# TensorE's instructions keep the order of the source, with grouped column-tiled products, from the second projection on

## The chip, the cores and the metric

One core of one Trainium2 chip runs the kernel. The metric is the device time of one execution in microseconds (us). Engines are named as the profile names them: PE is TensorE's matmul, PEld its weight load, DVE is VectorE, ACT is ScalarE, POOL is GpSimd, SP is SyncE, which here issues most DMAs.

## The reference

The input is x[1,256,1024]: 256 tokens, 1024 features, fp32. Two blocks run one after the other.

- The first block has one layer: an adaptive shift, scale and gate from a condition vector (the "ada" products); a state-space mixer (SSD, 32 heads in 4 groups, two chunks of 128 tokens); a sparse attention (NSA, 16 heads, with a compressed, a selected and a window branch); a gated sum of both; a router with 32 experts in 4 groups, two experts a token; a last RMS norm.
- The second block has two layers and a second sequence of 256 context tokens. Layer 0 is a grouped attention (16 heads on 4 key heads) of x over context and x, and of the context over itself, with a convolutional feed-forward for both. Layer 1 is a latent attention (MLA) of x over context and x with a feed-forward for x. A last RMS norm gives the output [1,256,1024].

```python
def first_block(...):                      # _hybrid_layer, one layer
    hn = _rmsnorm(h, norm1_g) * (1 + scale1) + shift1
    y_ssm = _mamba2_mixer(hn @ w_z, hn @ w_xbc, hn @ w_dt, ...) @ w_ssm_out
    y_nsa = _nsa_mixer(hn @ w_q, ..., hn @ w_gn, ...) @ w_nsa_out
    merged = sigmoid(hn @ w_gs) * y_ssm + sigmoid(hn @ w_ga) * y_nsa
    h = h + gate1 * (merged @ w_o)
    h = h + gate2 * _hier_moe(_rmsnorm(h, norm2_g) * (1 + scale2) + shift2, ...)
...
def mla_mixer(...):
    cq, ckv, k_rope = split(h @ w_in, [384, 640])
    q = rms_norm(cq, q_norm_g) @ w_uq
    kv = rms_norm(ckv, kv_norm_g) @ w_ukv
...
```

## The kernel before, in words

**Products.** Activations lie in SBUF feature-major, 128 features by 256 tokens a block. A product in nearly full fp32 precision is three matmuls in the type fp32r (`mm3`, lines 217 to 219): ACT casts a weight block to its high part (`whi`, line 198), DVE subtracts it for the low part (`wlo`, line 199), and PE adds high by high, low by high and high by low. `lin_fm` (line 221) keeps the weights stationary and streams 256 tokens; `lin_tm` keeps the activations stationary and streams up to 512 weight columns. These three lines, called the linear products below, are most of PE's work. Weights come by DMA on SP's queue into a ring of 14 buffers.

**Column- and row-tiled products.** Some products use only a part of the 128 by 128 array, and several of them sit side by side in it: the ada products (`ada_quad`, line 391) are four products of 32 columns each, written as a group of four for each of 8 slices of the weights; the experts' products (lines 1320 and 1342), the compressed scores (line 897) and the compression (line 850) are of the same kind. Attention's weighted sums (lines 989 and 1501) are pairs of 64 columns, its scores (944, 1690, 1713) pairs of 64 rows. Below, a burst is a run of such products with nothing of another kind, and not the same tile again, in between.

**The order.** The kernel is built on Tile, which collects the instructions of all engines and sets each engine's order itself, from its own estimate of when operands and buffers are ready; the order of the source sets only the priorities. The source is written as generators that `weave` and `mix` (lines 137 to 158) interleave: a main generator of linear products yields an estimated cost after each step, and fill generators (SSD, NSA, ada, attention, router) get a share of that cost. So the source has an interleaving of its own, in which a group is written whole; Tile's order before departs from it.

**The stages**, in order: the first projections (`first_act`, `project_tm`), the SSD's and convolution's inputs ("xbc"), the gates with SSD and NSA woven in (`ssd`, `nsa_compress` at line 832, `nsa_cmp_probs` at 890, `nsa_attend`), the two mixers' output products, the router, the experts with the context's attention and feed-forward of layer 0 woven in, then layer 0 for x (`layer0_x_attend`), its feed-forward with layer 1's context part, and layer 1 (`layer1_x`) with `mla_norm` (line 1741), `mla_kv_heads` and `mla_q_heads` and an attention (`attend`, line 1453) over them. `finish` makes the last norm. In `mla_norm` ACT copies a product out (line 1765) and squares it (1746), DVE and POOL make the reciprocal root (1747, 1749), DVE scales (1750) and PE transposes (1754). In a norm of x (`square_sums`, line 479) PE adds the squares up (491, 496), DVE and POOL make the root, PE broadcasts it (521), DVE and ACT make the normed activations (466 to 468), and the linear products follow.

**Buffers** that matter: PSUM has 8 banks. The first block gives 2 to the linear products, 1 to the ada products (`fl`), 2 to scores (`S`), 2 to `aux`, 1 to `acc`; the experts' stage 2, 2 (`S`), 2, 2; the layers of the second block 4 (`lin`, also the scores), 1, 2, 1.

Of the kernel before, what the change touches and what calls it, by code (L numbers as in the profile page):

```python
# [98 lines left out]
class Kernel:  # L99
# [915 lines left out]
    def tanh_gates(self, act, c0, sg):  # L1015
# [2 lines left out]
            self.A.activation(sg[:, m, :], ps, AF.Tanh, scale=0.5)  # L1018
        yield from self.lin_fm(self.I["w_in"][0], c0, D, act, ev)

    def mark(self, name):
        self.marks.append(name)

    def first_block(self, rb):
        V, A, T, I = self.V, self.A, self.T, self.I
        h = self.h
        act, pss = self.first_act(rb)
        self.mark("tm")
        self.drain(self.project_tm(act, pss))
        self.rope_tables()  # L1030
        self.ssd_dt()
        self.mark("xbc")
        self.load_vecs([3, 4, 5, 6, 7])
        for i in range(2):
            self.take_bias(self.fetch_bias(self.I["ada_b_2"][i]), self.ada2[i])
        prep = self.nsa_prepare()
        self.mix(self.project_xbc(act), (prep, 0.1))
        self.drain(prep)

        def nsa():  # L1040
            yield from self.nsa_compress()
            self.nsa_cmp_probs()
            yield 2.0
            yield from self.nsa_attend()
        ssg = self.sb("F", [P, 8, TOK], name="ssg")
        nsa_g, ssd_g, ada_g = nsa(), self.ssd(), self.ada_rest
        self.mark("ssg")
        self.mix(self.tanh_gates(act, 6992, ssg), (ssd_g, 0.7), (nsa_g, 0.35), (ada_g, 0.3))
        sga = self.sb("G", [P, 8, TOK], name="sga")
        self.mark("sga")  # L1050
        self.mix(self.tanh_gates(act, 8016, sga), (ssd_g, 0.6), (nsa_g, 0.35), (ada_g, 0.3))
        self.drain(ssd_g)
        self.mark("z")
        sums = [self.sb(f"cbm{i}", [P, 2, TOK], name="sums") for i in range(2)]
        self.mix(self.ssd_gate(act, sums), (nsa_g, 0.55), (ada_g, 0.3))
        self.drain(nsa_g)
        self.mark("norm")

        def ev_a(m, ps):
            V.scalar_tensor_tensor(sga[:, m, :], sga[:, m, :], 1.0, ps, OP.add, OP.mult)  # L1060
        norm = self.ssd_norm(sums)
        self.mix(self.lin_fm(I["w_nsa_out"][0], 0, D, self.nsa, ev_a), (norm, NORM), (ada_g, 0.2))
        self.drain(norm)
        self.mark("out")

        class Two:
            def __init__(self, ts):
                self.ts = ts

            def __getitem__(self, key):  # L1070
                _, k, s = key
                return self.ts[k // 8][:, k % 8, s]

        mh, ml = self.pair("B", [P, 8, TOK])

        def ev_s(m, ps):
            V.scalar_tensor_tensor(ssg[:, m, :], ssg[:, m, :], 1.0, ps, OP.add, OP.mult)
            V.tensor_tensor(sga[:, m, :], sga[:, m, :], ssg[:, m, :], OP.add)
            self.evict_split(mh[:, m, :], ml[:, m, :], sga[:, m, :])
        self.mix(self.lin_fm(I["w_ssm_out"][0], 0, D, (Two(self.y_hi), Two(self.y_lo)), ev_s), (ada_g, 0.3))  # L1080
        self.drain(ada_g)
        ctx = self.layer0_ctx_in()
        next(ctx)
        g = self.sb("s", [P, 8])
        V.tensor_scalar(g, self.ada1[:, 0, 16:24], 0.5, None, OP.mult)
        self.mix(self.residual(I["w_o"][0], (mh, ml), h, g), (ctx, CTXIN))
        self.drain(ctx)
        self.dbg("h1", h)
# [807 lines left out]
    def run(self):  # L1896
        with self.tc.tile_pool(name="sb", bufs=1) as self.pool:
            self.setup()
            self.h = self.sb("hx", [P, 8, TOK])
            self.ada1 = self.sb("ada1", [P, 1, 48])  # L1900
            self.ada2 = [self.sb(f"ada2{i}", [P, 2, 48]) for i in range(2)]
            for tag in SHARED:
                if tag == SHARED[tag]:
                    self.sb(tag, [P, 8, TOK])
            with self.phase(cw2=2, pb=5, pT=2), self.banks(lin=2, fl=1, S=2, aux=2, acc=1):
                first = [self.fetch_vecs(0)]
                x = self.fetch_tm(self.I["x"][0], "C", self.A)
                self.take_vecs([0], first)
                self.ada_stat()
                bias = self.fetch_bias(self.I["b_ada"][0])  # L1910
                first = [self.fetch_vecs(1)]
                self.turn_fm(x, self.h)
                self.load_constants(0)
                rb = self.sb("rb", [P, TOK])
                self.V.tensor_copy(rb, self.rms_bcast(self.h, 8, D))
                self.take_vecs([1], first)
                self.take_bias(bias, self.ada1)

                def rest():
                    yield from self.ada_first([1, 2])  # L1920
                    yield from self.ada_second(0)
                self.ada_rest = rest()
                self.first_block(rb)
            with self.phase(k4=4, m=3, fg=2, hT=2):
                with self.banks(lin=2, S=2, aux=2, acc=2):
                    self.load_constants(1)
                    self.mark("router")
                    ctx = self.layer0_ctx()
                    ada = self.ada_second(1, Q2)
                    self.mix(self.router(self.h), (ctx, 0.8), (ada, 0.5))  # L1930
                    self.drain(ada)
                    self.mark("experts")
                    self.mix(self.experts(), (ctx, 2.1))
                    self.mark("ctx rest")
                    self.drain(ctx)
                    self.mark("experts rest")
                    self.experts_rest()
                with self.banks(lin=4, fl=1, aux=2, acc=1):
                    self.mark("L0")
                    ada = self.ada_second(1, Q3)  # L1940
                    self.mix(self.layer0_x_attend(), (ada, 0.2))
                    self.drain(ada)
                    self.mark("L0 rest")
                    ctx = self.layer1_ctx()
                    self.mix(self.layer0_x_rest(), (ctx, 0.4))
                    self.drain(ctx)
                    self.mark("L1")
                    self.drain(self.layer1_x())
                    self.finish()


# [29 lines left out]
```

## Time and profile before

| | before |
|---|---|
| median of 3 runs | 1777.28 us (1777.13 to 1778.43) |
| the profiled execution | 1775.68 us, of it the profile's span 1773.9 us |
| PE busy | 1686.6 us (95%) |
| PEld busy | 1385.2 us (78%) |
| DVE busy | 1274.2 us (72%) |
| ACT busy | 913.8 us (52%) |
| POOL busy | 43.9 us (2%) |
| DMA | 381.54 MB, mean 215 GB/s |

A busy share is an average over stages with different limits. The stages lie in the profile at about these times: first projections to 78 us, xbc to 142, gates with SSD and NSA to 395, output products to 516, router to 577, context attention and experts to 1021, layer 0's projection to 1088, its attention to 1168, its feed-forward with layer 1's context to 1415, layer 1's latent projections to 1446, its attention to 1541, its feed-forward and the last norm to the end.

### The profile page before, as it was taken

The numbers are of one execution on the slowest core, as the hardware profiler recorded it, in microseconds if no ns is written. First come the engines' busy times: TensorE is split into PE (matmuls) and PEld (weight loads), VectorE is DVE, ScalarE is ACT, GpSimd is POOL, SyncE is SP. The second block draws the span as 40 slices with busy tenths as digits, with TensorE's granted clock in tenths as the row PEclk, the third lists the DMA queues.
The fourth block names the chain that finished last, engine by engine and source line by source line (L and its number), as shares of the span: only waits on it lengthen the run. The fifth ranks groups of instructions, "written<-read, shape, count | busy, mean of one in ns | idle before, by whom it ended". The sixth has DMA issues, their size and how long they took to land. (4 is left out here: it accounts for less than half of the span.)

```text
span 1773.9 us, 36446 instructions
## 1 busy us (share of the span) xinstructions
PE 1686.6 (95%) x12980; PEld 1385.2 (78%) x12980; DVE 1274.2 (72%) x3070; ACT 913.8 (52%) x1897; POOL 43.9 (2%) x48
## 2 busy tenths in 40 slices
PE   7999999999998999999999988999999989999998
PEld 3898767767876569888887644588999876789997
DVE  3997588566567677767666466968777788767876
ACT  2665445763443444434434253656665566556654
POOL 0000000010001000000000011000000000000000
PEclk9999999999999999999999989999999989989999
DMA  8756855847956897999999977334666432246662
GB/s 306 225 149 208 292 182 177 265 150 239 320 169 240 276 328 240 335 322 293 315 350 341 314 265 247 105 120 138 176 183 183 141 120 72 56 140 182 183 184 73
DMA packets 344962, 381.54 MB, mean 215 GB/s; under 512 B 27353, under 2 KB 298454, under 8 KB 344774
## 3 DMA queue, kind: packets, MB, share of 16 engines
q1 hardware_dynamic: 339456, 376.47, 67.7%
q10 hardware_dynamic: 5174, 1.97, 0.4%
q8 instruction: 104, 1.70, 0.4%
q14 instruction: 84, 0.69, 0.1%
q0 software_dynamic: 144, 0.71, 0.1%
HBM read 378.00 MB, written 1.05 MB: 214 GB/s over the span
## 5 line engine op out<-in xcount | busy, mean ns | idle before, releaser
L198 ACT CAST whi<-raw 128x512 fp32r<-128x512 f32 (+2 forms) x752 | 454.5, 610 | 403.5 <-PE lin L219 198.3
L199 DVE TENSOR_TENSOR wlo<-raw,whi 128x512 fp32r<-128x512 f32 (+2 forms) x752 | 503.8, 680 | 165.7 <-ACT whi L198 156.2
L217 PE MATMUL lin<-XA,whi 128*128 128x256 f32 x768 | 220.9, 288 | 1.4 <-ACT XA L467 1.4
L219 PE MATMUL lin<-XA,whi 128*128 128x256 f32 x768 | 219.6, 286 | 0.0
L218 PE MATMUL lin<-XA,wlo 128*128 128x256 f32 x768 | 219.4, 286 | 0.0
L217 PE MATMUL lin<-A,whi 128*128 128x256 f32 x576 | 167.8, 291 | 3.6 <-DVE k L600 1.9
L218 PE MATMUL lin<-A,wlo 128*128 128x256 f32 x576 | 164.6, 286 | 0.5 <-DVE wlo L199 0.5
L217 PEld LDWEIGHTS lin<-XA,whi 128*128 128x128 f32 x768 | 150.1, 195 | 2.7 <-ACT XA L467 2.5
L218 PEld LDWEIGHTS lin<-XA,wlo 128*128 128x128 f32 x768 | 149.7, 195 | 0.5 <-issue 0.4
L219 PEld LDWEIGHTS lin<-XA,whi 128*128 128x128 f32 x768 | 149.7, 195 | 0.3
L217 PEld LDWEIGHTS lin<-A,whi 128*128 128x128 f32 x576 | 110.6, 192 | 24.6 <-ACT whi L198 10.2
L219 PE MATMUL lin<-A,whi 128*128 128x256 f32 x448 | 128.5, 287 | 0.0
L217 PE MATMUL lin<-CA,whi 128*128 128x256 f32 x416 | 120.8, 290 | 0.0
L218 PE MATMUL lin<-CA,wlo 128*128 128x256 f32 x416 | 118.3, 284 | 0.0
L219 PE MATMUL lin<-CA,whi 128*128 128x256 f32 x416 | 118.0, 284 | 0.0
L218 PEld LDWEIGHTS lin<-A,wlo 128*128 128x128 f32 x576 | 110.7, 192 | 3.2 <-issue 1.6
L1624 ACT ACTIVATE cv<-lin,vecs 128x256 f32<-128x256 f32 x132 | 74.1, 561 | 62.0 <-PE lin L219 51.8
L219 PE MATMUL lin<-XB,whi 128*128 128x256 f32 x352 | 99.4, 286 | 0.1
L217 PE MATMUL lin<-XB,whi 128*128 128x256 f32 x352 | 98.7, 283 | 0.0
L218 PE MATMUL lin<-XB,wlo 128*128 128x256 f32 x352 | 98.4, 283 | 0.0
L1625 DVE SCALAR_TENSOR_TENSOR cv<-lin,vecs,cv 128x255 f32<-128x255 f32 x132 | 63.4, 480 | 44.8 <-ACT cv L1624 44.3
L219 PEld LDWEIGHTS lin<-A,whi 128*128 128x128 f32 x448 | 86.0, 192 | 1.3 <-issue 1.0
(534 smaller groups left out, 3826.1 us busy)
## 6 DMA issues: line engine op xcount, KB each, us to landing
raw<-in_ffn_w_up_dram SPq DMA_DIRECT2D x264, 256.0 KB
raw<-in_ada_w_dram SPq DMA_DIRECT2D x192, 256.0 KB
raw<-in_ffn_w_down_dram SPq DMA_DIRECT2D x132, 256.0 KB
raw<-in_w_in_dram SPq DMA_DIRECT2D x112, 256.0 KB
wx<-in_w_exp_gate_dram SPq DMA_DIRECT2D x112, 256.0 KB
wx<-in_w_exp_up_dram SPq DMA_DIRECT2D x112, 256.0 KB
wx<-in_w_exp_down_dram SPq DMA_DIRECT2D x112, 256.0 KB
raw<-in_w_ada_dram SPq DMA_DIRECT2D x96, 256.0 KB
```

Source lines behind the costliest of these rows:

```text
L198: self.A.copy(hi, raw)
L199: self.V.tensor_tensor(lo, raw, hi.bitcast(F32), OP.subtract)
L217: mm(out, whi, ahi, start=first, stop=False, skip_group_check=True)
L218: mm(out, wlo, ahi, start=False, stop=False, skip_group_check=True)
L219: mm(out, whi, alo, start=False, stop=last, skip_group_check=True)
L1624: A.activation(acc, ps, AF.Identity, bias=self.v(f"fb{i}", m), scale=self.v(f"fw{i}1", m))
L1625: V.scalar_tensor_tensor(acc[:, 1:], ps[:, 0:TOK - 1], self.v(f"fw{i}0", m), acc[:, 1:], OP.mult, OP.add)
```

## The change

A method `pin` enters and leaves Tile's manual schedule for TensorE alone. Between the two, PE's instructions stand in its queue in the order in which the source issues them; the other engines' orders are still Tile's, made anew around it. It is entered after `first_act`, left before `experts_rest`, entered after it and left before `finish`. No instruction is added or removed (11,765 on PE in both); from line 1026 on, the changed kernel's line numbers are 8 to 12 higher.

```diff
@@ -1018,6 +1018,14 @@
+    def pin(self, on=True):
+
+        if on:
+            self.pinned = self.tc.manual_schedule(engines={mybir.EngineType.PE})
+            self.pinned.__enter__()
+        else:
+            self.pinned.__exit__(None, None, None)
+
@@ -1025,6 +1033,7 @@
         act, pss = self.first_act(rb)
+        self.pin()
         self.mark("tm")
@@ -1934,7 +1943,9 @@
                     self.mark("experts rest")
+                    self.pin(False)
                     self.experts_rest()
+                    self.pin()
@@ -1946,6 +1957,7 @@
                     self.drain(self.layer1_x())
+                    self.pin(False)
                     self.finish()
```

PE's order in the SSD and NSA stage, an ada group (line 391) between SSD's products (707 to 730) and the linear products (217 to 219; `A_169` and `A_170` are the high and low activations). Before:

```order
L850 MATMUL acc<-raw,blk_2113 32x128 x2
L391 MATMUL fl<-raw,stat 32x512
L707 MATMUL aux<-k_2430,tri_r 128x512
L391 MATMUL fl<-raw,stat 32x512 x4
L724 MATMUL aux<-cst_129,k_2438 128x128 x4
L730 MATMUL aux<-bc,state 128x128 x4
L391 MATMUL fl<-raw,stat 32x512 x3
L217 MATMUL lin<-A_169,whi 128x256
```

Now:

```order
L850 MATMUL acc<-raw,blk_2111 32x128 x2
L850 MATMUL acc<-raw,blk_2115 32x128 x2
L391 MATMUL fl<-raw,stat 32x512 x8
L217 MATMUL lin<-A_169,whi 128x256
L218 MATMUL lin<-A_169,wlo 128x256
```

Eight products of one step, two groups of four, stood in three pieces, and stand in one.

PE's order a little later, around the softmax of the compressed scores (`nsa_cmp_probs`: scores 897, their transposes 903, the softmax on DVE and ACT, and the transposes of its result `scmp`, 924). Before:

```order
L737 MATMUL aux<-k_2784,xdt 64x128 x4
L897 MATMUL aux<-qT,kcmp 32x256 x4
L391 MATMUL fl<-raw,stat 32x512 x4
L903 MATMUL aux<-ident,scmpT 128x128 x2
L897 MATMUL aux<-qT,kcmp 32x256 x4
L391 MATMUL fl<-raw,stat 32x512 x3
L218 MATMUL lin<-A_169,wlo 128x256
...
L903 MATMUL aux<-ident,scmpT 128x128 x2
L219 MATMUL lin<-A_170,whi 128x256
...
L391 MATMUL fl<-raw,stat 32x512 x8
L217 MATMUL lin<-A_169,whi 128x256
...
L924 MATMUL aux<-ident,scmp 128x128 x4
```

Now:

```order
L737 MATMUL aux<-k_2786,xdt 64x128 x4
L897 MATMUL aux<-qT,kcmp 32x256 x4
L903 MATMUL aux<-ident,scmpT 128x128 x2
L897 MATMUL aux<-qT,kcmp 32x256 x4
L903 MATMUL aux<-ident,scmpT 128x128 x2
L924 MATMUL aux<-ident,scmp 128x128 x4
L391 MATMUL fl<-raw,stat 32x512 x8
L217 MATMUL lin<-A_169,whi 128x256
```

Between the second pair of transposes (903) and those of the result (924) stood 45 linear products and 8 ada products; now there is nothing, and the ada group comes behind.

PE's order at the start of layer 1 (`layer1_x`: products on the normed x `XA` with 288 and 384 columns, transposes of `mla_norm` at line 1754, 1763 in the changed kernel, products on the normed latent `comb`). Before:

```order
L218 MATMUL lin<-whi,XA_19384 128x288
...
L218 MATMUL lin<-whi,XA_19384 128x384
L1754 MATMUL aux<-ident,junk 128x128 x2
L219 MATMUL lin<-wlo,XA_19383 128x384
...
L1754 MATMUL aux<-ident,junk 128x128 x2
L219 MATMUL lin<-wlo,XA_19383 128x384
...
L217 MATMUL lin<-whi,comb_19520 128x512
L1754 MATMUL aux<-ident,junk 128x128 x3
L218 MATMUL lin<-whi,comb_19521 128x512
```

Now:

```order
L219 MATMUL lin<-wlo,XA_19388 128x288
L1763 MATMUL aux<-ident,junk 128x128 x4
L217 MATMUL lin<-whi,XA_19388 128x384
...
L219 MATMUL lin<-wlo,XA_19388 128x384
L1763 MATMUL aux<-ident,junk 128x128 x6
L217 MATMUL lin<-whi,comb_19525 128x512
```

The transposes of both norms stood 11 and more products of 384 or 512 columns behind the product that the norm works on; now they follow right behind its last matmul.

## Rows read from the trace of the kernel before

**Rows 1.** The page's first part: engine, busy us, share of the span, instructions.
```profile
PE 1686.6 (95%) x12980; PEld 1385.2 (78%) x12980; DVE 1274.2 (72%) x3070; ACT 913.8 (52%) x1897; POOL 43.9 (2%) x48
```

**Rows 2.** Windows: stretch, us, busy PE, PEld, DVE, ACT, POOL, PEclk, DMA share, GB/s.
```profile
215.00:290.00 75.00, 71.16 (x512) 50.98 (x510) 59.26 (x157) 29.73 (x77) 0.00 (x0) 0.98 0.61 197
268.00:291.00 23.00, 22.23 (x163) 15.58 (x158) 20.11 (x53) 10.15 (x23) 0.00 (x0) 1.00 0.58 187
366.00:396.00 30.00, 28.15 (x185) 17.17 (x183) 21.39 (x93) 18.46 (x60) 2.04 (x3) 1.00 0.43 131
590.00:648.00 58.00, 56.30 (x482) 29.75 (x474) 43.34 (x121) 29.84 (x91) 3.27 (x2) 1.00 1.00 320
625.00:1021.00 396.00, 387.79 (x3550) 323.15 (x3548) 269.63 (x614) 162.79 (x319) 0.70 (x1) 1.00 0.99 314
1088.00:1168.00 80.00, 75.50 (x481) 43.13 (x480) 64.74 (x165) 42.48 (x103) 3.46 (x3) 0.96 0.35 115
1415.00:1446.00 31.00, 24.55 (x130) 21.19 (x127) 22.84 (x70) 17.42 (x43) 2.87 (x5) 0.89 0.44 131
```

**Rows 3.** Timeline of PE, five places: start, us, line, operation, count [idle before, releaser].
```profile
151.60 1.04 PE L391 MATMUL fl<-raw,stat 128*32 128x512 f32 x2 [0.33 <-DMA raw<-in_w_ada_dram]
152.57 0.38 PE L217 MATMUL lin<-A,whi 128*128 128x256 f32 x1
...
163.95 0.28 PE L218 MATMUL lin<-A,wlo 128*128 128x256 f32 x1
164.07 0.28 PE L219 MATMUL lin<-A,whi 128*128 128x256 f32 x1
164.28 1.06 PE L391 MATMUL fl<-raw,stat 128*32 128x512 f32 x8
165.27 0.38 PE L217 MATMUL lin<-A,whi 128*128 128x256 f32 x1
...
232.83 0.64 PE L897 MATMUL aux<-qT,kcmp 128*32 128x256 f32 x8
233.28 0.61 PE L391 MATMUL fl<-raw,stat 128*32 128x512 f32 x4
...
240.64 1.92 PE L391 MATMUL fl<-raw,stat 128*32 128x512 f32 x16
242.49 0.39 PE L217 MATMUL lin<-A,whi 128*128 128x256 f32 x1
...
1120.45 0.39 PE L1713 MATMUL lin<-klo,qTx 64*128 64x512 f32 x1
1120.77 0.44 PE L1493 MATMUL aux<-ident,prob 128*128 128x128 f32 x2
```

**Rows 4.** Tile scmp, DVE's and ACT's instructions: count, ns min/median/max, start.
```profile
L913 DVE TENSOR_TENSOR scmp<-scmp,cst x2: 418/418/419, 242.3 to 242.7; 128x256 f32<-128x256 f32 x2
L908 DVE TENSOR_REDUCE s<-scmp x1: 686/686/686, 237.9 to 237.9; 128x32 f32<-128x512 f32 x1
L910 ACT ACTIVATE scmp<-scmp x1: 632/632/632, 241.3 to 241.3; 128x512 f32<-128x512 f32 x1
```

**Rows 5.** Timeline of layer 1's first latent norm.
```profile
1429.51 0.29 PE L219 MATMUL lin<-wlo,XA 128*128 128x288 f32 x1
...
1431.30 0.54 POOL L1749 TENSOR_TENSOR s<-s,mhalf 128x1 f32<-128x1 f32 x1 [13.71 <-DVE s L1747]
...
1432.37 0.41 PE L1754 MATMUL aux<-ident,junk 128*128 128x128 f32 x2 [0.66 <-DVE junk L1750]
```

**Rows 6.** Timeline of PE in the norm of x ahead of layer 1.
```profile
1418.19 0.72 PE L521 MATMUL aux<-k,ones 128*128 128x256 f32 x2 [1.65 <-DVE k L518]
...
1420.03 0.85 PE L217 MATMUL lin<-whi,XA 128*128 128x288 f32 x2 [1.11 <-ACT XA L467]
```

**Rows 7.** Timeline at the start of xbc: one bias issue, and the transpose of its result.
```profile
79.53 0.38 ACTq L375 DMA_DIRECT2D stg<-in_ada_b_dram  x1
...
82.33 0.26 PE L381 MATMUL aux<-ident,stg 48*128 48x48 f32 x1
```

## The prediction

> **What bounds the kernel now.** I read the page's busy times first, then the windows by stage, then PE's timeline and its waits. PE is busy 1686.6 of 1773.9 us [rows 1]; DVE and ACT stand at 72% and 52%, and the weight loads overlap the matmuls. By stage it is the same: PE is busy 71.2 of 75 us in the SSD and NSA stage and 387.8 of 396 among the experts, where the DMA engines are full too (0.99) [rows 2]. So time is gained where PE's instructions take less of PE, and lost where PE, with its order fixed, stands before an instruction whose operand is late. Both have to be summed. The exception is layer 0's attention, where DVE is busy 64.7 of 80 us [rows 2] and its chain of reductions sets the steps.
>
> **The gain.** A burst of column tiles costs PE the same whether it holds one tile or four. One ada tile with its two passes (fp32) goes from 151.60 to the linear product at 152.57, 0.97 us; four tiles from 164.28 to 165.27, 0.99 us [rows 3]. The step into the tiled form shows as 164.07 to 164.28, 0.21 where linear products follow each other by 0.12 [rows 3], so 0.09 more. Two bursts in a row go from 240.64 to 242.49, 1.85 [rows 3], so one more burst costs 1.85 - 0.99 = 0.86, and the way back 0.99 - 0.86 = 0.13. I take 0.1 a change.
>
> I counted bursts in PE's order, before and now: line 391 82 and 64; 1320 120 and 112; 1342 60 and 56; 1501 84 and 80; 989 and 944 19 and 16, 11 and 8 (those of 256 columns); 1690 22 and 16; 1713 68 and 48; 850 18 and 16. A burst of 256 columns in fp32 takes 0.45 (232.83 to 233.28 [rows 3]), taken as 0.43, half of 0.86. One of line 1713 takes 0.32 with its change of form, 0.23 without (1120.45 to 1120.77 [rows 3]).
> - Line 391: 18 x 0.86 = 15.5.
> - The 256-column ones: 8 + 4 + 4 + 3 + 3 + 6 = 28 x 0.43 = 12.0. Line 1713: 20 x 0.23 = 4.6. Line 850: 2 x 0.2 = 0.4.
> - Changes of form fall from 475 to 352: 123 x 0.1 = 12.3.
>
> Together 44.8 us of PE's time. Not all of it reaches the end. Layer 0's attention holds 9.2 of it, and I credit 6, because DVE is behind. The context's attention among the experts (590 to 648, PE 56.3 of 58 us [rows 2]) holds 9.7; its scores have two banks, so a step waits for the reduction and exponential of the step before, and I credit 6. That leaves 37.9.
>
> The Trainium skill, TensorEngine Tiling (Array Packing), Key Properties, says that changing the tiling mode drains TensorE. By that rule the count of changes pays as counted here; the trace agrees, with its 0.09 us on the way in.
>
> **The loss.** Tile had put linear products between a producer and PE's next use of it. The source's order has fewer of them, so PE waits there. I priced each place by the chain's length or by the cover that goes, whichever is less.
> - *Start of xbc, 3.0.* Five transposes of constants and two of biases now stand in one block ahead of the linear products. The second bias is issued at 79.53 and its transpose runs about 3 us later [rows 7]; 25 linear products x 0.12 stood between.
> - *Softmax of compressed scores, 7.* Cover was 45 linear products and a double ada burst; now none. The chain is one operation of 0.42, two of 0.42 (line 913), the reductions and scalings of 0.69 (four like line 908) and the exponential of 0.63 [rows 4], some 5 us with its small steps. The compression's chain ahead of it loses 12 linear products, 1.4; the turn of the scores 0.6. Bounds 5 and 11.
> - *End of SSD, 3.* From 268 to 291, DVE is busy 20.1 of 23 us [rows 2]; 41 linear products that filled this leave it. Bounds 2 and 5.
> - *End of NSA, 4.* 366 to 396 has PE busy 28.2 of 30 [rows 2], of it 38 linear products and two double ada bursts that leave, while DVE's 21.4 stay. Bounds 2 and 8.
> - *Norms, 10.1.* A norm of x without cover idles PE 1.65 and 1.11 [rows 6], 2.8 and more. Five others had cover and lose part or all of it: 8.5 (context, router, context feed-forward, final, layer 1's context; 1.7 each). The SSD's norm loses 13 linear products, 1.6.
> - *Router, 3; layer 0's projection, 2; end of its attention, 3* (24 linear products leave it, 2.9).
> - *Experts, 5.* Three pairs of small products lose cover that the other units keep; DMA is full there (0.99 [rows 2]), which hides part. Bounds 0 and 10.
> - *Layer 1, 11.9.* The first latent norm's transposes run 2.86 us after the start of the last matmul that they need (1429.51 to 1432.37 [rows 5]), POOL's 0.54 among it; all of it was covered but 0.66. Now 2.5 is bare. The second norm is a chain of the same kind, 2.8. The turns of keys and queries lose 1.2, 2.0 and 1.5, and the attention's tail 16 linear products, 1.9. Bounds 6 and 17.
>
> Sum of losses: 3 + 7 + 3 + 4 + 10.1 + 3 + 2 + 3 + 5 + 11.9 = 52.0. Less 37.9 of gain, +14.1 us. No instruction is added, DMAs keep their count, and SP's and POOL's orders change only by following PE. The profiled execution took 1775.7, so 1789.8; it stands 1.6 below the median, so I give **1791** for the median. What a measurement can tell from no change is about 0.2%, 3.6 us.
>
> **Rivals.**
> - *Faster.* DVE and ACT are ordered anew around PE's fixed order, so a chain's operations no longer stand behind weight splits that PE's old order wanted first. Place: the softmax and the latent norms. For it: the softmax's first reduction starts at 237.9 and its exponential only at 241.3 [rows 4], with 0.69 of work between, so the chains were stretched on purpose under their cover; and a wait of PE lets the splits and the DMAs run ahead, which shortens the next wait. Against: I already count the softmax at its bare length, and PE has too little idle time to catch up in. If losses are half, 26, the result is 26 - 37.9 = -12, 1765. It decides at losses under 34.
> - *Slower still, by the clock.* The granted clock is 0.89 in the 31 us of layer 1's latent norms and 0.98 to 1.00 in most stages [rows 2]. That stage holds the norm's waits of rows 6, so behind waits of this kind PE ran partly at the lower of its two levels, 1.2 instead of 2.4 GHz; 0.11 x 31 = 3.4 us for one such group of waits. Five to six new groups of the like (softmax, latent norms, three norms) cost 17 to 20: 1809. Against: the stretches of 590 to 1021 show 1.00 in spite of their short waits. The Trainium skill, TensorE: Matmul & The Clock Gate, Why this matters for your kernels, asks that gaps between bursts of matmuls be kept short, as the clock falls in them; it speaks against this change by the same mechanism.
> - *No difference.* Gains and losses are near each other: losses of 34 to 42 give it, 1777. Or DMA sets the experts' pace so that neither the context attention's 6 nor the experts' 5 count; this alone moves the sum by 1.
> - That the order isn't what the change says is ruled out: PE's order now is the source's, and the groups stand whole.
>
> **How the numbers follow.** The forecast gets 0.37, the clock rival 0.15, no difference 0.13, the faster one 0.35. So faster by over 0.2% 0.35, within it 0.13, slower 0.52. The losses carry bounds of 30 to 75 when their places lean together, so the sum lies between -8 and +37 without the clock. The likeliest case's own range is 1781 to 1806. With the rivals I give 1756 to 1820: below it lies a full gain of 22 us, that is losses under 16, above it both the clock and the upper bounds.
>
> **What would show it.** Right: PE's busy time falls by 35 to 45 us to about 1645, while its idle time grows by over 50; waits of PE on line 1763's operand of 2 us or more, and one of about 5 us before line 924; the window of layer 1's attention and norms longer by about 10 us; the context attention shorter by about 6; the granted clock near 0.98. Wrong: if the busy time falls as said and the waits at these places are under half of the prices, the faster rival holds. If the busy time doesn't fall, the burst's price is wrong. If the mean clock falls to 0.97 or less and the waits are as priced, the clock rival holds.

## The result, and the profile after

The changed kernel takes 1966.74 us (median of 4 runs, 1960.13 to 1972.15) against 1777.2 us before: ratio 1.1066, interval 1.1028 to 1.1104. It is 190 us slower; the forecast was 14 us slower. The profiled execution's span is 1962.5 us. The page's busy times and its slices of the granted clock:

```profile
PE 1717.5 (88%) x12980; PEld 1422.1 (72%) x12980; DVE 1287.8 (66%) x3070; ACT 920.2 (47%) x1897; POOL 43.2 (2%) x48
...
PEclk9999887999989899999999978998999988999999
```

Against [rows 1], PE's busy time has not fallen by 45 us but risen by 30.9, and the span outside it has grown from 87.3 to 245.0 us, by 157.7. Together that is the span's 188.6. DVE and ACT did the same work as before (1274.2 and 913.8 us there).

The windows of the changed kernel, cut at the same points of the program as the table below (columns as in [rows 2]):

```profile
78.90:334.70 255.80, 211.95 (x1592) 175.66 (x1590) 173.97 (x397) 106.65 (x219) 0.00 (x0) 0.88 0.53 160
334.70:452.30 117.60, 106.79 (x802) 80.08 (x798) 73.20 (x263) 79.06 (x198) 10.96 (x13) 0.99 0.58 181
...
549.50:608.50 59.00, 46.96 (x311) 38.24 (x309) 31.30 (x69) 22.89 (x43) 1.39 (x2) 0.86 0.42 124
...
668.20:740.60 72.40, 56.79 (x520) 32.77 (x520) 43.72 (x121) 31.02 (x92) 3.27 (x2) 0.91 0.72 231
740.60:1133.30 392.70, 366.38 (x3357) 312.13 (x3354) 251.13 (x562) 152.31 (x283) 0.70 (x1) 0.99 0.96 304
...
1209.20:1299.90 90.70, 63.62 (x434) 36.70 (x434) 65.11 (x159) 42.50 (x102) 3.41 (x2) 0.87 0.32 106
...
1563.50:1598.40 34.90, 24.47 (x129) 21.40 (x128) 21.16 (x62) 14.39 (x34) 1.78 (x3) 0.80 0.33 99
1598.40:1718.00 119.60, 100.06 (x495) 68.29 (x494) 79.72 (x220) 60.80 (x144) 1.08 (x2) 0.93 0.17 55
```

| stage, between the same instructions | us before | us after | PE not busy, before | after | clock before | after |
|---|---|---|---|---|---|---|
| xbc, gates, SSD | 212.4 | 255.8 | 7.3 | 43.9 | 0.99 | 0.88 |
| rest of NSA | 105.3 | 117.6 | 3.2 | 10.8 | 1.00 | 0.99 |
| output products | 89.8 | 97.2 | 2.8 | 6.0 | 1.00 | 0.96 |
| to the router | 43.5 | 59.0 | 2.2 | 12.0 | 1.00 | 0.86 |
| router | 56.7 | 59.7 | 5.2 | 9.5 | 0.94 | 0.91 |
| context's attention | 61.5 | 72.4 | 1.7 | 15.6 | 1.00 | 0.91 |
| experts | 373.0 | 392.7 | 8.2 | 26.3 | 1.00 | 0.99 |
| layer 0's projection | 65.7 | 75.9 | 10.2 | 18.8 | 0.92 | 0.82 |
| layer 0's attention | 77.5 | 90.7 | 4.5 | 27.1 | 0.96 | 0.87 |
| layer 1's latent products | 26.8 | 34.9 | 5.4 | 10.4 | 0.87 | 0.80 |
| layer 1's attention | 98.0 | 119.6 | 4.2 | 19.5 | 0.98 | 0.93 |

No stage is faster; the stages left out (the feed-forwards and the start) add 23 us. What PE waited for, in the list of its waits in the changed kernel (total us, number of waits, longest):

```profile
PE aux L706 <- DVE k L700: 20.1, 11, 4.2
PE aux L1583 <- DVE pr L1460: 18.2, 2, 11.2
PE aux L521 <- DVE k L518: 14.9, 8, 3.2
PE aux L1763 <- DVE junk L1759: 13.0, 5, 2.9
PE acc L1510 <- DVE pT L1504: 11.0, 12, 1.7
...
PE aux L362 <- DMA x_tm<-in_ctx_dram: 6.5, 1, 6.5
...
PE S L1699 <- ACT prob L1483: 6.1, 1, 6.1
PE aux L924 <- DVE scmp L920: 5.8, 1, 5.8
...
PE acc L989 <- ACT pT L977: 5.3, 3, 3.5
PE lin L217 <- DVE k L600: 4.7, 5, 2.0
```

In the same list of the kernel before the same places are short, and line 706 stands there with two waits:

```profile
PE aux L521 <- DVE k L518: 7.5, 9, 1.7
...
PE aux L1574 <- DVE pr L1570: 2.5, 1, 2.5
...
PE aux L1754 <- DVE junk L1750: 2.1, 5, 0.7
...
PE aux L706 <- DVE k L700: 0.8, 2, 0.5
```

Nearly every wait is on DVE or ACT (161 and 51 us in all, 40 and 24 before): a product waits for a chain of a few operations that PE itself started just before. The exception is line 362, one of the longest single waits and in no price of the prediction: the transposes of the context's input stand right behind the last output product and wait 6.5 us for a transfer from DRAM, where the old order had linear products. That is two thirds of what the stage "to the router" lost of PE's time (12.0 against 2.2). Two places show the chains, in the changed kernel's timeline. First the softmax of the compressed scores:

```profile
254.88 0.44 PE L903 MATMUL aux<-ident,scmpT 128*128 128x128 f32 x2 [0.71 <-DVE scmpT L900]
261.11 1.09 PE L924 MATMUL aux<-ident,scmp 128*128 128x128 f32 x4 [5.80 <-DVE scmp L920]
```

This one was in the prediction (5 us). Then one of eleven waits of the SSD's decay products, which was not:

```profile
268.38 0.60 PE L687 MATMUL aux<-ident,xs 128*128 128x128 f32 x4
269.02 0.62 ACT L198 CAST whi<-raw 128x512 fp32r<-128x512 f32 x1 [11.14 <-PE aux L687]
269.67 0.69 DVE L199 TENSOR_TENSOR wlo<-raw,whi 128x512 fp32r<-128x512 f32 x1 [6.74 <-ACT whi L198]
270.28 0.69 DVE L689 TENSOR_TENSOR xdt<-aux,dt 128x512 f32<-128x512 f32 x1
...
271.10 0.69 DVE L199 TENSOR_TENSOR wlo<-raw,whi 128x512 fp32r<-128x512 f32 x1
271.71 0.69 DVE L693 TENSOR_TENSOR k<-xdt,s 128x512 f32<-128x512 f32 x1
272.31 0.68 DVE L700 TENSOR_TENSOR k<-cst,dta_hi 128x512 fp32r<-128x512 f32 x1
...
273.14 0.76 PE L706 MATMUL aux<-k,tri_r 128*128 128x512 f32 x1 [4.16 <-DVE k L700]
```

PE transposes `xs` (687) and then stands at line 706, whose operand comes from line 700 on DVE. DVE, in its own order, first has a weight split that waits for ACT's cast (of its 6.74 us idle, 0.7 lie inside PE's wait), then the operation on the transposes, a second split and a scaling (693), and only then line 700. So most of PE's 4.16 us is DVE at work, some 1.3 of them on the two splits. The linear products that could run meanwhile stand behind 706 in PE's queue.

### The profile page after: what moved, and what is told of

Read it like the earlier page. It is cut to its first block, busy times and chain, and to the rows that moved or that the text cites. A ratio compares the mean times of both kernels' runs of the same rounds, so it can differ in the third digit from the quotient of the medians.

```text
span 1962.5 us, 36432 instructions
## 1 busy us (share of the span) xinstructions
PE 1717.5 (88%) x12980; PEld 1422.1 (72%) x12980; DVE 1287.8 (66%) x3070; ACT 920.2 (47%) x1897; POOL 43.2 (2%) x48
## 5 line engine op out<-in xcount | busy, mean ns | idle before, releaser
L217 PE MATMUL lin<-A,whi 128*128 128x256 f32 x576 | 171.7, 298 | 5.9 <-DVE k L600 4.7
L217 PEld LDWEIGHTS lin<-A,whi 128*128 128x128 f32 x576 | 115.3, 200 | 26.0 <-issue 12.0
L219 PE MATMUL lin<-A,whi 128*128 128x256 f32 x448 | 131.1, 293 | 0.0
L218 PEld LDWEIGHTS lin<-A,wlo 128*128 128x128 f32 x576 | 115.3, 200 | 2.9 <-DVE wlo L199 2.6
L217 PE MATMUL lin<-XB,whi 128*128 128x256 f32 x352 | 101.1, 287 | 7.8 <-ACT XB L211 7.8
L219 PE MATMUL lin<-XB,whi 128*128 128x256 f32 x352 | 101.5, 288 | 1.1 <-DVE XB L212 0.5
L217 PEld LDWEIGHTS lin<-CA,whi 128*128 128x128 f32 x416 | 80.6, 194 | 15.4 <-ACT whi L198 6.7
```

The lines of the kernel that those rows point to most:

```text
L217: mm(out, whi, ahi, start=first, stop=False, skip_group_check=True)
L218: mm(out, wlo, ahi, start=False, stop=False, skip_group_check=True)
L219: mm(out, whi, alo, start=False, stop=last, skip_group_check=True)
```

## The experiments

**Which part costs what.** Three kernels keep PE's order in one part alone.

```diff
 # first block alone
                 self.first_block(rb)
+                self.pin(False)
...
 # router to layer 0's attention alone: pin() at mark("router"), pin(False) at mark("L0 rest")
 # layer 1 alone: pin() at mark("L1")
```

> TensorE's order kept in the first block alone, from the second projection to the router. Theory A (the 190 us are local waits, stage by stage, with the clock that falls behind them): the router's first products start 79 us later in the changed kernel (608.5 against 529.5), so this kernel takes 1777 + 79 = about 1856 us, and its waits in the SSD stage are those of the changed kernel (about 44 us of idle PE there against 7). Theory B (one late stream carries through: weights fall behind once and stay behind): the first block alone costs most of it, over 120 us, or nearly nothing, under 40.

> The order kept from the router to the end of layer 0's attention alone (not in the stage that the changed kernel leaves free too). Theory A: the stretch is 61.6 us longer in the changed kernel (726.1 against 664.5 from the router's first products to the end of the feed-forward's first part), so about 1839 us. Theory B: under 1800 or over 1880.

> The order kept in layer 1 alone. Theory A: the rest of the changed kernel is 48 us longer, so about 1825 us, a little less since the feed-forward of layer 0 is free here. Theory B: under 1800. The three parts together give 1777 + 79 + 62 + 48 = 1966 by theory A; by theory B they don't add up to it.

Measured against 1774.85 us in these runs: 1848.18 (ratio 1.0414, interval 1.0381 to 1.0448), 1840.39 (1.0371, 1.0334 to 1.0407) and 1809.05 (1.0194, 1.0161 to 1.0227). That is +73, +66 and +34, together 173 of 190; the stretch that none of them holds, layer 0's feed-forward with layer 1's context part, is some 15 us longer in the changed kernel. In the first kernel the stages behind the router have their old lengths (373 us for the experts, as before). So theory A holds: the loss is local, made of waits at their own places. The first block was 6 below its expectation of 79, and layer 1 14 below its 48; 10 of the 48 belonged to that feed-forward.

**The grouping without the order.** Groups are issued whole, everything else stays with the scheduler. A group's last product goes first, so the group waits for its last weight.

```diff
+    def together(self, *calls):
+        with self.tc.manual_schedule(engines={mybir.EngineType.PE}):
+            calls[0]()
+            with self.tc.high_priority(offset=3000):
+                for f in calls[1:]:
+                    f()
...
-            for j in range(4):
-                c = 2048 * q + 512 * j
-                self.T.matmul(acc[32 * j:32 * j + 32, :], ...)
+            self.together(*[lambda j=j: self.T.matmul(acc[32 * j:32 * j + 32, :], ...) for j in (3, 0, 1, 2)])
```

> The order is left to the scheduler, but each group of tiled products is issued whole (ada, experts' up and down, scores of layer 0 and of the context, the weighted sums of those attentions): the first of a group keeps its priority, the others follow it at once. Bursts of the ada line fall from 82 to 64 as in the changed kernel, the experts' from 204 to 192, layer 0's scores from 68 to 51, and changes of form from 475 to 433. By the prediction's prices that is 18 x 0.86 + 12 x 0.43 + 17 x 0.23 + 42 x 0.1 + 1 = about 30 us of TensorE's time. Theory A (grouping itself gains, the lost cover costs): 1747 to 1762 us, faster by 15 to 30, TensorE's busy time lower by 25 to 30. Theory B (a group costs what it saves, since it waits for its last weight or the burst's price is wrong): within 5 us of 1777.

Measured: 1774.39 us, ratio 0.9997, interval 0.9973 to 1.0022. Its page:

```profile
PE 1659.4 (94%) x12980; PEld 1381.2 (78%) x12980; DVE 1273.3 (72%) x3070; ACT 915.0 (52%) x1897; POOL 42.1 (2%) x48
```

PE's busy time fell by 27.2 us against [rows 1], where the prices gave 30: the prices of a burst and of a change of form have the right size. (The granted clock was 0.976 here against 0.983: PE was busy for 70 us at the lower of its two levels, 50 before, which by an estimate hides 9 or 10 us more of saving.) But the span is 1771.9, so the time outside it grew from 87.3 to 112.5. Theory A holds for PE's busy time, and theory B for the kernel, on the first of its two grounds: the grouped products now wait for their weights. These rows stand in the list of PE's waits here:

```profile
PE fl L391 <- DMA raw<-in_ada_w_dram: 8.2, 7, 3.1
...
PE acc L1349 <- DMA wx<-in_w_exp_down_dram: 2.8, 3, 1.8
...
PE fl L391 <- DMA raw<-in_w_ada_dram: 2.3, 2, 1.2
```

The ada products (391) wait 11.4 us for weights, 1.1 before, and the experts' products 5.9, 0.2 before; that is 16 of the 25 us by which the time outside grew. Whether a group waits for its last weight or PE came too early for any of them isn't separated. By stage, SSD ends 6.1 us earlier, what lies from there to the end of the output products takes 4.3 longer; layer 0's attention is 4.2 shorter, its projection and the experts 4.1 longer.

**The groups where the run was ahead.** The same helper, used for the ada products during SSD and NSA and in layer 0's attention alone.

> The kernel before, order left to the scheduler, with groups issued whole only where the run with all groups whole was ahead of it: the ada products while SSD and NSA are woven in (that stage ended 6 us earlier there) and layer 0's scores and weighted sums (4 us). Theory A (the saved time stays where the next stage doesn't wait for weights): 5 to 10 us faster than the kernel before, 0.3 to 0.6%. Theory B (what is saved is waited for later, at the output products, whatever the stage): within 3 us.

Measured: 1773.72 us, ratio 0.9986, interval 0.997 to 1.0002. The interval holds no change; theory B fits, and a gain of a few us can't be excluded. PE's busy time fell by 13.4 us and the span by 2.0; the ada products wait 7.6 us for weights, 1.1 before. No kernel here was clearly faster than the one before.

**The clock.** Idle transposes fill five kinds of waits in the changed kernel; they compute nothing that is used.

```diff
+    def warm(self, out, n):
+        for _ in range(n):
+            self.T.transpose(out, self.ident, self.ident)
...
                     flat = pseg.rearrange("p h i -> p (h i)")
+                    self.warm(flat[:, 0:P], 10)
...
```

> The changed kernel, with transposes of the identity that nothing uses put in front of five kinds of waiting products, into the PSUM tile that the waiting product overwrites: 10 before each SSD decay product (16 times), 45 before the transposes after the softmax of the compressed scores, 30 before the first transposes of each call of the grouped attention's heads, 20 before the latent norms' transposes, 12 before each norm's broadcast. A transpose takes 0.11 us. They fill waits that hold some 80 of the 230 us of idle time and remove none. Theory A (the granted clock falls behind the waits, and that is about half of the loss): the granted clock of the SSD stage rises from 0.88 to 0.95 or more, and the kernel is faster than the changed one by 25 to 60 us, 1905 to 1940. Theory B (the loss is the waits themselves, the lower clock only falls on time that is waited anyway): within 10 us of the changed kernel, or slower by up to 20 where the transposes outlast a wait.

Measured: 1946.35 us (ratio to before 1.0974, interval 1.0879 to 1.1069). That is 20 us below the changed kernel, or 16 by the two ratios, since the kernel before took 1770.44 in these runs; the interval still touches the changed kernel's, so the stages decide. The page's busy times and the SSD stage's window:

```profile
PE 1750.2 (90%) x13629; PEld 1466.0 (76%) x13629; DVE 1285.9 (66%) x3070; ACT 920.3 (47%) x1897; POOL 42.8 (2%) x48
```
```profile
77.90:325.90 248.00, 218.57 (x1797) 187.22 (x1795) 173.46 (x397) 106.58 (x219) 0.00 (x0) 0.97 0.54 166
```

The clock rose as theory A said, from 0.88 to 0.97 in the SSD stage and from 0.941 to 0.969 over the span. There are 649 added transposes; at 0.11 us they are 71 us of the 1750.2, so the kernel's own instructions took 1679, 38 us less than in the changed kernel. Of these 38, 16 to 20 reached the end, under the forecast of 25 to 60; the transposes also delay where they outlast a wait, and how much that took is not separated. So the lower clock is a real part of the loss, not only slow work inside time that is waited anyway, and by these estimates the smaller part.

**Cover spread more finely.** The linear products give way after 6 matmuls instead of 24.

```diff
-                if kg + n < nk:
-                    yield n * 0.66
+                    if k < n - 1:
+                        yield 0.66
+                if kg + n < nk:
+                    yield 0.66
...
```

> The changed kernel, with the linear products' generator giving way after every 6 matmuls instead of after every 24, so that the source's order has them spread more evenly between the other generators' steps. Theory A (the cover is there but in lumps: 24 matmuls, 2.9 us, stand at one step of a chain and none at the next): waits of the SSD's decay products fall from 24 us to under 10, idle time of the kernel by 40 or more, 1890 to 1930 us. Theory B (the order of DVE and ACT, or too little work in all, keeps TensorE waiting): within 15 us of the changed kernel, or slower for its 12 more changes of form and more.

Measured: 1946.86 us (ratio to before 1.0977, interval 1.0894 to 1.1061), 16 to 20 below the changed kernel, between the two theories. Waits of the SSD's decay product went from 20.1 to 13.7 us, its stage from 255.8 to about 241; the stages in which little but a chain is left did not move (layer 0's attention 90.8 us, 90.7 in the changed kernel).

**Other engines in the source's order too.**

```diff
-            self.pinned = self.tc.manual_schedule(engines={mybir.EngineType.PE})
+            self.pinned = self.tc.manual_schedule(engines={mybir.EngineType.PE, self.nc.vector.engine})
```

> VectorE keeps the order of the source too, in the same stretches as TensorE. Theory A (TensorE waits since DVE's order, made from estimates, doesn't fit TensorE's, with a weight split that waits for its buffer ahead of the operation that TensorE waits for): faster than the changed kernel by 20 us or more. Theory B (the source's order itself lacks cover): no faster, and slower by 20 or more since DVE now waits in the source's order too.

> ScalarE keeps the order of the source too, as well as VectorE and TensorE. Theory A as for VectorE alone: faster than the changed kernel by 20 us or more, and faster than with VectorE alone. Theory B: slower than the changed kernel.

Measured: 2508.33 us (ratio 1.4143, interval 1.4035 to 1.4251) and 2660.85 us (1.5003, 1.4889 to 1.5117). Waits of PE with DVE in the source's order:

```profile
PE lin L218 <- DVE wlo L199: 280.8, 126, 12.3
PE lin L219 <- DVE wlo L199: 60.1, 23, 12.4
...
PE aux L706 <- DVE k L700: 22.1, 11, 2.3
```

Theory A falls. DVE's order from the scheduler is what still feeds PE in the changed kernel: in the source's order weights are split just ahead of their use, and PE waits 341 us for them. The waits at line 706 stay as they were, 22.1 us, so the source's order of DVE doesn't remove them. Whether some third order of DVE would shorten them wasn't run.

**A chain given cover in the source.** The generator of the compressed scores gives way before line 924.

```diff
         V.tensor_tensor(s3, s3, sm.unsqueeze(2).to_broadcast([P, 32, 16]), OP.mult)
+        yield 2.0
         tp = self.ps("aux", [P, 2, 2, P])
...
```

> The changed kernel, with the generator of the compressed scores giving way between the softmax and the transposes of its result, so that the source has an ada group, two lots of linear products and SSD products there. Theory A (a wait is the cover that the source lacks at its own place): the wait of 5.8 us before line 924 falls under 1 and the kernel is 5 to 10 us faster than the changed one (1967), the clock's share included. Theory B (the wait is only moved, for the next chain has less cover): within 3 us.

Measured: 1949.86 us (ratio 1.0978, interval 1.0939 to 1.1016), 16 to 17 below the changed kernel. PE's wait of 5.8 us before line 924 is gone (0.7 us are left before the weight load of these transposes), and the SSD stage ends 8.9 us earlier; theory A. Of the rest, some 5 us lie in layer 1's attention, which this edit doesn't touch: the kernels with kept order scatter by some us (the changed one by 12 between its runs).

**Weighted sums a step later**, in the three attentions of the second block.

```diff
+            if done:
+                combine(done.pop())
+                yield nkt * 0.5
             if m >= 2:
                 i, t0 = steps[m - 2]
                 turn(i, t0)
                 yield 0.88
                 if t0 + nt == 2:
-                    combine(i)
-                    yield nkt * 0.5
+                    done.append(i)
...
```

> The changed kernel, with the weighted sums of each head pair in the three attentions of the second block issued one step later, behind the next scores, so that they no longer follow the transposes whose copies they need. Theory A: the waits of line 1510, 18 us over 22 places in the changed kernel, fall under 6 and the kernel is 10 to 20 us faster than the changed one, about 1950. Theory B (DVE's reductions set the steps, so the wait goes to the next product): under 5 us faster.

Measured: 1961.73 us (ratio 1.1045, interval 1.1005 to 1.1084), 4 to 5 us below, within the scatter. The weighted sums' own waits did as asked, from 19.1 us to 5.8 in all, and layer 0's attention went from 90.7 to 84.0 us; but elsewhere others took their place, as in this list of PE's waits:

```profile
PE aux L1830 <- DVE room L1460: 11.0, 8, 2.0
PE S L1705 <- ACT prob L1483: 7.9, 3, 6.1
...
PE aux L1338 <- DVE k L1335: 6.9, 6, 3.2
```

The first of them was 3.7 us in the changed kernel (line 1824 there). So a repaired place hands part of its wait on: A in layer 0, B in the others.

**The three repairs together.**

> The three repairs of the source's order together: linear products in steps of 6, the compressed scores giving way, the later weighted sums. Theory A: the gains add, 20 + 7 + 14, about 1925 us. Theory B: they overlap, over 1935. Either way it stays over 100 us behind the kernel before, since chains of the norms, of layer 0's heads and of layer 1 keep no cover.

Measured: 1939.7 us (ratio 1.0921, interval 1.0882 to 1.0959), 27 below the changed kernel (26 by the ratios) where the parts were 20, 17 and 5; this one's interval lies clear of the changed kernel's. The parts overlap (theory B), and 162 us of the loss stay.

## Why the prediction was right and wrong

- **Direction.** Slower was forecast as the likeliest, and it is slower; but 1967 lies far above the range of 1756 to 1820.
- **The gain's prices held in size.** PE's busy time fell by 27.2 against 30 where groups alone were changed. In the changed kernel the gain of 44.8 can't be seen directly, since the clock hides it; so the sign named for a wrong price, a busy time that doesn't fall, was itself wrong.
- **The step that failed is the sum of losses, 52.0.** Measured is 157.7 us more in which PE isn't busy. Where a single chain was priced, the price was of the right size: softmax 5 of the 7 (measured 5.8, minus the 1.0 before), the latent norms 2.5 and 2.8 a chain (measured 2.2 to 2.9). But each of these norms has two such chains, one for every 128 tokens, and PE stands at both: four waits of 10.3 us in all, 1.7 before, where the sum has two of 5.3. What failed is the list of places and how often each comes. I looked for spots where linear products had visibly stood between a producer and its consumer in the old order, and priced these. But a fixed order makes PE wait at every chain that its own next instruction needs, and most of them repeat: the SSD's decay products, priced only for the end of SSD (3), wait 23.6 us at lines 706 and 707; layer 0's heads (1583) 27.8 in five waits, against 7.3 in five before; the weighted sums (1510) 19.1 in 21, against 1.8 in two; the context's scores (1699) 6.1; the context's input (362) 6.5. The stages show the gap best: SSD with the softmax and the start of xbc was priced at 13 and lost 36.6 of PE's time; layer 0's attention at 3 and lost 22.6; the context's attention at nothing, lost 13.9. The three kernels that keep part of the order show that this is local and adds.
- **What I credited.** I let 6 of 9.2 us count in layer 0's attention because DVE sets the steps, and 6 of 9.7 in the context's. Both stages became longer, by 13.2 and 10.9. In layer 0's attention DVE was busy for four fifths of the stage, and the old order fed its steps earlier: DVE's 64 us of work there filled 77.5 us before, and 65 us fill 90.7 now.
- **The clock was a rival, not a term, at 17.** The granted clock fell from 0.983 to 0.941. PE's busy time rose by 30.9 where by the prices 44.8 of work had gone, so about 76 us of busy time came in. By an estimate from the traces some 60 of them are the clock's: PE was busy for 180 us at the lower of its two levels, 50 before, and the linear products follow each other by 0.213 us there instead of 0.120. The rest is open; 105 more waits may be part of it, since a linear product shows as busy for 0.28 us, and ahead of a wait all of it counts, not the 0.12 to the start of a next one. The filled waits show that a part of it is real (38 us for the places filled). The size failed because I counted six groups of waits; PE stands for over 0.4 us in 149 places of the changed kernel, and in 66 of the one before. The Trainium skill, TensorE: Matmul & The Clock Gate, Why this matters for your kernels, asks for short gaps between bursts of matmuls. The trace agrees, with 0.88 in the SSD stage, whose longest gap is 5.8 us, and 0.97 when the gaps are filled.
- **The rivals.** The faster one (DVE and ACT ordered anew around PE, losses halved) is ruled out: waits were three times the sum, and giving DVE the source's order made them worse. The clock rival came nearest, with its mechanism right and its size a third (17 to 20 of some 60); but its condition, waits as priced, didn't hold. The remark that DMA may hide what the experts lose didn't hold: 19.7 us longer, DMA share 0.96 instead of 0.99.

## What to carry to other kernels

When a hand-written order replaces a scheduler's, price it by walking the new order and asking of each instruction which chain on another engine it needs and how many instructions stand since that chain began; the places where the old order showed cover are only part of them, and those that repeat cost most. A saving on the busiest engine, even of the right size (27 us here), reaches the end only where the next thing isn't another engine's work or a weight; group instructions first, and see whether the time outside the engine grows by as much. Here an engine at 95% got there by early issue of small chains, so an order that keeps groups whole should be asked for at the groups, not over the whole program.

## What the runs showed of the hardware

The granted clock fell with many short waits too, not only behind a few long ones: in the SSD stage of the changed kernel waits of up to 5.8 us, 44 of 256 us in all, went with a clock of 0.88. In this part of it no wait is longer than 1.8 us, and 3.6 of 30 us are idle:

```profile
200.00:230.00 30.00, 26.40 (x233) 19.40 (x233) 17.43 (x32) 12.11 (x22) 0.00 (x0) 0.89 0.81 264
```

The experts' stage, with 26 of 393 us in waits of up to 1.7 us, kept 0.99. Transposes that do nothing, put into such waits, brought the SSD stage back to 0.97, and the kernel became 16 to 20 us faster with 649 instructions more.
